# A hybrid decoder layer: the steps of w_down's second half at which turned tiles are taken apart and put together

## The chip, the core and the metric

The kernel runs on one core of a Trainium2 chip. The metric is the device time of one execution in microseconds (us). TensorE multiplies matrices, VectorE and ScalarE work on tiles element by element, GpSimd is used here for a few transfers, and SyncE issues most transfers (DMAs). Each engine works through its own instructions in order, and semaphores tie the engines together.

## What is computed

The layer holds 256 tokens of width 2048. A mixer (chunked SSD scan beside dilated attention) comes first; the change lies in the last product of the MLP behind it. What matters of the reference:

```
def squared_relu_mlp(u, w_up, w_down):
    hdn = jax.nn.relu(jnp.einsum('bsd,df->bsf', u, w_up))
    return jnp.einsum('bsf,fd->bsd', hdn * hdn, w_down)
...
        ff = squared_relu_mlp(rmsnorm(h, norm_mlp_pre[i]), w_up[i], w_down[i])
        h = h + rmsnorm(ff, norm_mlp_post[i])
```

The hidden width is 8192. The kernel takes it in two halves of 4096: w_up's half first, then the rows of w_down that belong to it.

## The kernel before, in words

**Products in two parts.** A float32 operand is split into a high part, which ScalarE rounds (`split`, L150, tiles `hi`), and the rest, which VectorE subtracts (L151, tiles `lo`). TensorE then forms hi·hi, lo·hi and hi·lo. Weights pass through five `hi` and five `lo` buffers (`BUFS = 5`), so that a split can be written only when TensorE is through with the one five splits before.

**Units and steps.** `unit` forms two blocks of 512 columns of w_down at a time. It takes the inner dimension in steps of two 128-row tiles. A plain step fetches two weight tiles, splits two, and feeds 24 matmuls of 512 columns. A step "by seven" (`seven`) does a 2x2 block product with seven products in place of eight: it has four splits, three additions of weights on VectorE, and 21 matmuls. It also needs sums of activations (`sums_of_acts`, three additions or subtractions with the names `r<-r` and a split with the name `ua<-r`), which are made one step ahead. The first unit of w_down's second half has the order 0, 1, 3, 2, 6, 4, 5, 8, 7, 9, 10, 11, 12, 13 of inner pairs, where 3, 6, 8, 9, 11 and 13 go by seven. In steps counted from 0: steps 2, 4, 7, 9, 11 and 13 go by seven, the others are plain. After step 13 the last two pairs (14 and 15) follow as plain ones; I call them the last steps.

**Turned tiles.** The blocks of w_up leave tokens on the partitions, and w_down needs features there. Each of the four blocks that the last unit of w_up leaves is therefore turned (`turned`) in two parts. Taking it apart: ScalarE applies relu and square (L1522, L1523) and writes the 16-bit halves apart (L1515, `ha<-hb` or `ha<-wpost`, 128x1024), and SyncE issues a transposing DMA (L1525). Putting it together, called landing here: ScalarE joins the halves again (L1515, `ha<-hb` or `ha<-wpost`, 128x2x512) and rounds the result (L150, `ah_3798`), and VectorE subtracts (L151, `al_3799`). Two tuples say at which steps of a unit this stands: `TURNS` before the step's own work, `LANDS` after it. In w_down's units both parts are placed exactly: `in_line` orders them after the splits recorded so far.

**What follows the last landing.** When no turned tile is left, `more_in_place` runs: the tile of the halves becomes a further place for fetched weights (`ha`), and two rows of norm weights are loaded. The weights of the last steps begin with that place, so their first fetch waits for the fourth landing, and three more are chained behind it.

Of the kernel before, what the change touches and what calls it, by code (L numbers as in the profile page):

```python
# [54 lines left out]
V_SEVENS = (1, 3, 5, 6)  # L55
QK_SEVENS = (1, 3, 5, 6)
PAIRS_AHEAD = 4
TURNS = ((1, 2, 4, 5), (3, 4, 8, 9))
LANDS = ((0, 3, 4, 6), (0, 6, 7, 10, 11))


def constants():
# [18 lines left out]
def hymba_layer(ctx: ExitStack, tc: tile.TileContext, x, norm_mix_pre, w_in, conv_w, conv_b, dt_bias, a_log,  # L81
# [99 lines left out]
    room = {}  # L181
# [13 lines left out]
    def beside_up(raws, turn, halves=None):  # L195

        room["sums"] = [v[:, k:k + KB] for k in range(0, NK // 2, KB) for v in att[1]]
        b = hp.tile([P, NT, NB], F32, name="hb")
        room["shared"] = [[b[:, t] for t in range(NT)],
                          [hp.tile([P, NB], F32, name="wpost", bufs=2) for _ in range(NT)]]  # L200
        room["last"] = deque([room["shared"][1].pop(), hp.tile([P, NB], F32, name="junk")])
        room["shared"][1].append(room["last"][0])
        a = hp.tile([P, 3 * KB, NB], F32, name="ha")
        in_a = [a[:, k:k + KB] for k in range(0, 3 * KB, KB)]
        halves = in_a.pop(0) if halves is None else halves
        room["halves"] = deque(halves[:, i].bitcast(U16) for i in range(KB))
        room["raw"], room["turn"], room["acts"], room["chain"] = [*raws, *in_a], turn, act_u, True
        room["of_halves"], room["of_a"] = halves, in_a
        sums_of.clear()

    def beside_down():

        a = hp.tile([P, 3 * KB, 2, S], F32R, name="ha")
        room["sums"] = [a[:, k] for k in range(3 * KB)]
        room["raw"], room["turn"], room["acts"] = [mws[2]], 0, part
        room["halves"] = deque(mws[0][:, t, c0:c0 + NB].bitcast(U16) for t in range(NT) for c0 in (0, NB))
        room["then"] = [(4, halves_beside_down), (2, more_beside_down), (0, all_beside_down)]
        sums_of.clear()

# [65 lines left out]
    def blocks_of(n):  # L285
        return n if isinstance(n, tuple) else (n * NB, (n + 1) * NB)
# [57 lines left out]
    def drain():  # L344
        while waiting:
            pump()
# [3 lines left out]
    def pump_beside(exact=False):  # L350

        if not beside:
            return
        work = beside.popleft()
        room["exact"] = exact
        with tc.issue_after(newest["act"].ins):
            next(work)
        flying.append(work)

    def land_beside(exact=False):  # L360

        room["exact"] = exact
        if flying:
            with tc.issue_after(newest["act"].ins):
                next(flying.popleft(), None)
        if "then" in room and len(beside) + len(flying) <= room["then"][0][0]:
            room["then"].pop(0)[1]()
            if not room["then"]:
                room.pop("then")
# [49 lines left out]
    def sums_of_acts(k):  # L419

        if k in sums_of:
            return sums_of[k]
        places = room["sums"][2 * len(sums_of):][:2]
        h_, l_, r = room["acts"](k * KB)
        with tc.high_priority(offset=AHEAD):
            a, c = (tmp().rearrange("p (i s) -> p i s", s=P) for _ in range(2))
            ah_, al_ = (v[:, r:r + KB].bitcast(F32).rearrange("p j (t s) -> p j t s", t=NT) for v in (h_, l_))
            nc.vector.tensor_tensor(a.rearrange("p (j t) s -> p j t s", t=NT), ah_, al_, op=ALU.add)
            nc.vector.tensor_tensor(c[:, 0:2], a[:, 0::3], a[:, 1:2].to_broadcast([P, 2, P]), op=ALU.subtract)
            nc.vector.tensor_tensor(c[:, 2], a[:, 0], c[:, 1], op=ALU.add)  # L430
            nc.vector.tensor_tensor(c[:, 3], a[:, 2], c[:, 2], op=ALU.subtract)
            ch, cl = (v.rearrange("p b (t s) -> p (b t) s", t=NT) for v in places)
            split(ch, cl, c)
        sums_of[k] = ch, cl
        return ch, cl

    def seven(src, ca, cb, k, acc, more, first, last):


        ch, cl = sums_of_acts(k)  # L440
        h_, l_, r = room["acts"](k * KB)
        with tc.high_priority(offset=AHEAD):
            raw_a = fetch_next(src, k * KB, ca)
            raw_b = fetch_next(src, k * KB, cb, pair_of(src, ca, k))
            e, t4 = sum_tile(), tmp()
            add_in_line(e[:, 1], raw_a[:, 0], raw_b[:, 0])
            add_in_line(e[:, 0], e[:, 1], raw_b[:, 1], ALU.subtract)
            hl_a = parts()
            split_in_line(*hl_a, raw_a)
            add_in_line(t4, e[:, 1], raw_a[:, 1])  # L450
            hl_e = parts()
            split_in_line(*hl_e, e)
            hl_b = parts()
            split_in_line(*hl_b, raw_b)
            hl_t = parts()
            split_in_line(*(v[:, 0] for v in hl_t), t4)

        def block(j, t):
            return tuple(v[:, r + j, t * P:(t + 1) * P] for v in (h_, l_))

        def summed(i):
            return ch[:, i], cl[:, i]

        for dst, (a_h, a_l), (hi, lo), j, own in (
                (more[0], block(0, 0), hl_a, 0, True), (acc[0], block(1, 0), hl_a, 1, False),
                (more[1], summed(1), hl_e, 0, True), (more[2], summed(2), hl_e, 1, True),
                (more[3], summed(0), hl_b, 0, True), (acc[1], summed(3), hl_b, 1, False),
                (acc[2], block(1, 1), hl_t, 0, False)):
            nc.tensor.matmul(dst, a_h, hi[:, j], start=own and first, stop=False)  # L469
            nc.tensor.matmul(dst, a_h, lo[:, j], start=False, stop=False)  # L470
            nc.tensor.matmul(dst, a_l, hi[:, j], start=False, stop=own and last)  # L471
# [30 lines left out]
    def unit(src, n, order, last, acc, more, combine, lag=0, at_end=(None, None), first=True, ending=None,  # L502
             ready=None, halves=None):


        cols = blocks_of(n)
        sevens = [k for k, by_seven in order if by_seven]
        for i, (k, by_seven) in enumerate(order):
            if i in TURNS[len(order) > 7]:
                pump_beside(len(order) > 7)  # L510
            if i + 1 < len(order) and order[i + 1][1]:
                sums_of_acts(order[i + 1][0])
            if by_seven:
                if k == sevens[0]:
                    drain()
                    if ready:
                        ready()
                seven(src, *cols, k, acc, more, k == sevens[0], k == sevens[-1])
            else:
                for b in range(2):  # L520
                    row_tiles(src, cols[b], [k], acc[b::2], room["acts"], first and i == 0, False,
                              fetch=fetch_next)
            if i in LANDS[len(order) > 7]:
                land_beside(len(order) > 7 and i > 0)
            if k == sevens[-1]:
                combine(more)
        for b in range(2):
            if b and ending:
                ended.append(ending(cols[b], last, acc))
            else:  # L530
                row_tiles(src, cols[b], last, acc[b::2], room["acts"], False, True, lag if b else 0, at_end[b],
                          fetch=fetch_last if b else fetch_next, halves=halves if b else None)
# [956 lines left out]
    def out_of_place():  # L1489

        yield from copies(in_dram, of_h, 4)
        beside_up([*tiles_of(mws[0], (0, NB)), mws[2]], -2 * RAWS, mws[1])
        for k in UP_SEVENS:
            sums_of_acts(k)
            yield
# [73 lines left out]
    def complete(n):  # L1569
        def at_end(t, acc):  # L1570
            m = mw_at(t, columns(n))
            nc.vector.tensor_add(m, acc, m)
            junk = hp.tile([P, NB], F32, name="junk")
            nc.scalar.activation(junk, m, AF.Square, accum_out=ssq[:, t, n:n + 1])
            nc.vector.tensor_mul(m, m, wpost[n])
            if n == 2:
                first3[t] = sums_but_last(ssq, t)
        return at_end
# [6 lines left out]
    def more_in_place():  # L1585
# [5 lines left out]
        for n in range(2):  # L1591
            load_wpost(norm_mlp_post, n)

    room["then"] = [(0, more_in_place)]
    unit(w_downs[1], 0, orders[("down", 1), 0], (14, 15), acc, more,
         lambda x: combine_onto(0, x), 0, (complete(0), complete(1)))
    room["chain"] = False
# [36 lines left out]
```

## Time and profile before

| | us |
|---|---|
| median of 3 runs (1441.72 to 1447.8) | 1443.69 |
| the profiled execution | 1444.83 |
| its span in the trace | 1442.9 |
| TensorE busy in it | 1432.2 (99%) |

The span is the time from the first to the last instruction in the trace; the profiled execution's own time has 1.93 us around it. Busy time of TensorE counts matmuls that overlap in its pipeline: each lasts 0.39 us and they start about 0.23 us apart, so a matmul that starts late shows as a larger distance between starts before it shows as idle time.

### The profile page before, as it was taken

How to read it: one execution, taken by the hardware profiler on the slowest of the kernel's cores; microseconds unless marked ns; L12 is line 12 of the kernel's file. 1: busy time of each engine (PE TensorE's matmuls, PEld its weight loads, DVE VectorE, ACT ScalarE, POOL GpSimd, SP SyncE). 2: the span in 40 equal slices, each digit the busy share in tenths (PEclk: the TensorE clock that was granted, in tenths of full speed). 3: DMA queues.
4: the chain of work that ended last, by engine and by line, in shares of the span. 5: the costliest groups of instructions: out<-in, count | busy, mean ns of one | idle time of the engine just before them, and what ended most of it. 6: DMA issues, size and time to landing. Idle time of an engine off the chain costs nothing.

```text
span 1442.9 us, 20235 instructions
## 1 busy us (share of the span) xinstructions
PE 1432.2 (99%) x6930; PEld 1204.6 (83%) x6930; DVE 1297.6 (90%) x1881; ACT 1003.1 (70%) x1407; POOL 162.8 (11%) x244
## 2 busy tenths in 40 slices
PE   9999999999999999999999999999999999999998
PEld 8888888888888888888888888888888888887886
DVE  7788888988999778689988999999889999999998
ACT  7577669666666666656667669978565799978664
POOL 0301110121111000011100011010111011111000
PEclk9999999999999999999999999999999999999999
DMA  8977656756888648588976799799888899998954
GB/s 266 282 211 227 188 171 184 246 176 193 220 244 259 198 119 253 176 259 261 274 230 218 203 340 291 206 253 254 256 251 272 253 266 298 247 274 251 323 194 146
DMA packets 201926, 340.30 MB, mean 236 GB/s; under 512 B 45616, under 2 KB 48544, under 8 KB 201824
## 3 DMA queue, kind: packets, MB, share of 16 engines
q1 hardware_dynamic: 174304, 279.72, 61.7%
q0 software_dynamic: 19648, 45.63, 15.5%
q10 hardware_dynamic: 7872, 13.68, 2.9%
q8 instruction: 54, 0.88, 0.2%
q14 instruction: 48, 0.39, 0.1%
HBM read 327.39 MB, written 49.84 MB: 261 GB/s over the span
## 4 chain that ended last, share of the span: by engine, by line
PE 64%; DVE 5%; ACT 4%; DMA 2%; issue 2%; SPq 0%; ACTq 0%; DVEq 0%
PE acc L383 9%; PE acc L384 9%; PE acc L382 9%; PE acc L470 5%; PE acc L471 5%; PE acc L469 5%; PE acc L540 4%; PE ps L383 2%; PE ps L384 2%; PE ps L382 2%; PE acc L543 2%; ACT hi L150 2%; DVE lo L151 2%; PE ps L469 2%; PE ps L470 2%
## 5 line engine op out<-in xcount | busy, mean ns | idle before, releaser
L151 DVE TENSOR_TENSOR lo<-raw,hi 128x1024 fp32r<-128x1024 f32 (+1 forms) x390 | 473.2, 1218 | 79.0 <-ACT hi L150 77.2
L150 ACT ACTIVATE hi<-raw 128x1024 fp32r<-128x1024 f32 (+1 forms) x390 | 406.5, 1048 | 174.1 <-PE acc L384 51.2
L540 PE MATMUL acc<-ua,hi 128*128 128x512 f32 x520 | 141.2, 400 | 0.0
L150 ACT ACTIVATE hi<-e 128x1024 fp32r<-128x1024 f32 x66 | 69.9, 1059 | 53.6 <-DVE e L275 49.9
L540 PEld LDWEIGHTS acc<-ua,hi 128*128 128x128 f32 x520 | 91.3, 189 | 14.0
L382 PE MATMUL acc<-hi,ua 128*128 128x512 f32 x228 | 90.0, 395 | 0.0
L383 PE MATMUL acc<-lo,ua 128*128 128x512 f32 x228 | 89.2, 391 | 0.0
L384 PE MATMUL acc<-hi,ua 128*128 128x512 f32 x228 | 89.0, 390 | 0.0
L382 PE MATMUL acc<-hi,sh 128*128 128x512 f32 x220 | 86.7, 394 | 0.0
L383 PE MATMUL acc<-lo,sh 128*128 128x512 f32 x220 | 85.7, 390 | 0.0
L384 PE MATMUL acc<-hi,sl 128*128 128x512 f32 x220 | 85.7, 389 | 0.0
L543 PEld LDWEIGHTS acc<-ua,lo 128*128 128x128 f32 x520 | 76.5, 189 | 8.9
L151 DVE TENSOR_TENSOR lo<-e,hi 128x1024 fp32r<-128x1024 f32 x66 | 80.4, 1218 | 0.9 <-ACT hi L150 0.7
L543 PE MATMUL acc<-ua,lo 128*128 128x256 f32 x520 | 78.8, 281 | 0.0
L470 PE MATMUL acc<-lo,ah 128*128 128x512 f32 x180 | 70.1, 390 | 0.0
L471 PE MATMUL acc<-hi,al 128*128 128x512 f32 x180 | 70.0, 389 | 0.0
L469 PE MATMUL acc<-hi,ah 128*128 128x512 f32 x180 | 70.0, 389 | 0.0
L151 DVE TENSOR_TENSOR lo<-ha,hi 128x1024 fp32r<-128x1024 f32 x48 | 58.3, 1219 | 3.7 <-ACT hi L150 3.5
L540 PE MATMUL acc<-uc,hi 128*128 128x512 f32 x208 | 61.4, 405 | 0.0
L150 ACT ACTIVATE hi<-ha 128x1024 fp32r<-128x1024 f32 x48 | 50.3, 1050 | 9.4 <-PE acc L384 5.7
L469 PE MATMUL acc<-hi,ua 128*128 128x512 f32 x137 | 53.5, 390 | 0.0
L471 PE MATMUL acc<-hi,ua 128*128 128x512 f32 x137 | 53.3, 389 | 0.0
(578 smaller groups left out, 3724.7 us busy)
## 6 DMA issues: line engine op xcount, KB each, us to landing
raw<-in_w_in_dram SPq DMA_DIRECT2D x154, 512.0 KB, 4.4
raw<-in_w_down_dram SPq DMA_DIRECT2D x70, 512.0 KB, 5.7
raw<-in_w_up_dram SPq DMA_DIRECT2D x65, 512.0 KB, 4.8
raw<-in_w_out_dram SPq DMA_DIRECT2D x38, 512.0 KB, 5.3
raw<-pair SPq DMA_DIRECT2D x59, 256.0 KB, 4.5
pair<-in_w_up_dram POOLq DMA_DIRECT2D x56, 256.0 KB, 6.4
pair<-in_w_down_dram POOLq DMA_DIRECT2D x52, 256.0 KB, 6.0
ha<-in_w_up_dram SPq DMA_DIRECT2D x25, 512.0 KB, 6.0
```

The source lines that it names most:

```text
L150: return (nc.scalar.activation(hi, src, AF.Copy), nc.vector.tensor_tensor(lo, src, hi.bitcast(F32), op=ALU.subtract))
L151: nc.vector.tensor_tensor(lo, src, hi.bitcast(F32), op=ALU.subtract))
L382: nc.tensor.matmul(dst[:, cs], a_h[:, r, ts], hi[:, j, cs], start=begin and j == 0, stop=False)
L383: nc.tensor.matmul(dst[:, cs], a_h[:, r, ts], lo[:, j, cs], start=False, stop=False)
L384: product[t] = nc.tensor.matmul(dst[:, cs], a_l[:, r, ts], hi[:, j, cs], start=False, stop=end and j == KB - 1)
L469: nc.tensor.matmul(dst, a_h, hi[:, j], start=own and first, stop=False)
L470: nc.tensor.matmul(dst, a_h, lo[:, j], start=False, stop=False)
L471: nc.tensor.matmul(dst, a_l, hi[:, j], start=False, stop=own and last)
L540: nc.tensor.matmul(acc[f], hi[:, j, f * P:(f + 1) * P], u(k0 + j), start=k0 + j == 0, stop=False, skip_group_check=True)
L543: nc.tensor.matmul(acc[f][:, 0], lo[:, j, f * P:(f + 1) * P], u(k0 + j)[:, 0], start=False, stop=k0 + j == NK - 1, skip_group_check=True)
```

## The change

A third pair of tuples is added for w_down's second half, and the unit chooses its pair by a number in `room` in place of the length of the order. Tiles one and two are taken apart at steps 3 and 4 as before, tiles three and four at steps 9 and 10 in place of 8 and 9. The landings stand behind steps 7, 8, 11 and 12 in place of 6, 7, 10 and 11. The units of w_up keep the first pair and those of w_down's first half the second.

```diff
-TURNS = ((1, 2, 4, 5), (3, 4, 8, 9))
-LANDS = ((0, 3, 4, 6), (0, 6, 7, 10, 11))
+TURNS = ((1, 2, 4, 5), (3, 4, 8, 9), (3, 4, 9, 10))
+LANDS = ((0, 3, 4, 6), (0, 6, 7, 10, 11), (0, 7, 8, 11, 12))
...
-        room["of_halves"], room["of_a"] = halves, in_a
+        room["of_halves"], room["of_a"], room["table"] = halves, in_a, 0
...
+        room["table"] = 1
...
+        table = room.get("table", 0)
...
-            if i in TURNS[len(order) > 7]:
-                pump_beside(len(order) > 7)
+            if i in TURNS[table]:
+                pump_beside(table > 0)
...
-            if i in LANDS[len(order) > 7]:
-                land_beside(len(order) > 7 and i > 0)
+            if i in LANDS[table]:
+                land_beside(table > 0 and i > 0)
...
+    room["table"] = 2
     unit(w_downs[1], 0, orders[("down", 1), 0], (14, 15), acc, more,
```

TensorE and GpSimd have the same instructions in the same order as before. Three places show how the others move. From line 209 on the changed kernel's line numbers are one, two or three higher than before (L275 becomes L276, L1515 becomes L1517, L1522 becomes L1524).

First, VectorE at the start of step 7 (`raw` are its weights, `e` their sums), before:

```order
L430 TENSOR_TENSOR r<-r 128x128
L151 TENSOR_TENSOR lo<-raw,hi 128x1024
L431 TENSOR_TENSOR r<-r 128x128
L151 TENSOR_TENSOR al_3799<-ha,ah_3798 128x4x128
L275 TENSOR_TENSOR e<-raw 128x512
L275 TENSOR_TENSOR e<-e,raw 128x512
L151 TENSOR_TENSOR ua<-r,ua 128x512
L151 TENSOR_TENSOR lo<-raw,hi 128x1024
L275 TENSOR_TENSOR r<-e,raw 128x512
```

and with the change:

```order
L431 TENSOR_TENSOR r<-r 128x128
L151 TENSOR_TENSOR lo<-raw,hi 128x1024
L432 TENSOR_TENSOR r<-r 128x128
L276 TENSOR_TENSOR e<-raw 128x512
L276 TENSOR_TENSOR e<-e,raw 128x512
L151 TENSOR_TENSOR ua<-r,ua 128x512
L151 TENSOR_TENSOR lo<-raw,hi 128x1024
L276 TENSOR_TENSOR r<-e,raw 128x512
```

The subtraction of the first landing (`al_3799`) no longer stands ahead of step 7's additions; it comes after its last split, beyond these rows.

Second, ScalarE from the last split of step 7 (`hi<-r`) to the first of step 9 (`hi<-ha`); the two `hi<-uc` are those of step 8. Before:

```order
L150 ACTIVATE hi<-r 128x512
L1515 ACTIVATE ha<-hb 128x2x512
L150 ACTIVATE ah_3798<-ha 128x4x128
L1522 ACTIVATE wpost<-wpost,rmlp 128x512
L1523 ACTIVATE wpost<-wpost 128x512
L150 ACTIVATE ua<-r 128x512
L1515 ACTIVATE ha<-wpost 128x1024
L150 ACTIVATE hi<-uc 128x1024 x2
L1522 ACTIVATE wpost<-wpost,rmlp 128x512
L1523 ACTIVATE wpost<-wpost 128x512
L1515 ACTIVATE ha<-wpost 128x1024
L150 ACTIVATE hi<-ha 128x1024
```

With the change:

```order
L150 ACTIVATE hi<-r 128x512
L1517 ACTIVATE ha<-hb 128x2x512
L150 ACTIVATE ah_3798<-ha 128x4x128
L150 ACTIVATE ua<-r 128x512
L150 ACTIVATE hi<-uc 128x1024 x2
L1517 ACTIVATE ha<-hb 128x2x512
L150 ACTIVATE ah_3798<-ha 128x4x128
L1524 ACTIVATE wpost<-wpost,rmlp 128x512
L1525 ACTIVATE wpost<-wpost 128x512
L1517 ACTIVATE ha<-wpost 128x1024
L150 ACTIVATE hi<-ha 128x1024
```

Before, the second landing and the taking apart of the third tile stand ahead of step 8's splits; now the first landing stands there, and the second landing and the third tile follow them, ahead of step 9's. The fourth tile is taken apart between step 9's splits and step 10's.

Third, VectorE at the fourth landing, where `lo<-uc` are the splits of step 12 and `e<-ha` begins step 13. Before:

```order
L151 TENSOR_TENSOR lo<-r,hi 128x512
L151 TENSOR_TENSOR al_3799<-ha,ah_3798 128x4x128
L428 TENSOR_TENSOR r<-ah_3798,al_3799 128x512
L151 TENSOR_TENSOR lo<-uc,hi 128x1024
L429 TENSOR_TENSOR r<-r 128x256
L151 TENSOR_TENSOR lo<-uc,hi 128x1024
L430 TENSOR_TENSOR r<-r 128x128
```

With the change:

```order
L151 TENSOR_TENSOR lo<-r,hi 128x512
L429 TENSOR_TENSOR r<-ah_3798,al_3799 128x512
L151 TENSOR_TENSOR al_3799<-ha,ah_3798 128x4x128
L430 TENSOR_TENSOR r<-r 128x256
L151 TENSOR_TENSOR lo<-uc,hi 128x1024
L431 TENSOR_TENSOR r<-r 128x128
L151 TENSOR_TENSOR lo<-uc,hi 128x1024
L432 TENSOR_TENSOR r<-r 128x128
L151 TENSOR_TENSOR al_3799<-ha,ah_3798 128x4x128
L276 TENSOR_TENSOR e<-ha 128x512
```

The fourth landing's subtraction has moved behind both splits of step 12. SyncE's queue from there, before (from the third transposing DMA):

```order
L1525 DMA_TRANSPOSE wpost<-ha 128x8x128
L164 DMA uc<-in_w_down_dram 128x2x512 x2
L1525 DMA_TRANSPOSE wpost<-ha 128x8x128
L164 DMA ha<-in_w_down_dram 128x2x512
L159 DMA ha<-pair_93 128x512
L160 DMA ha<-in_w_down_dram 128x512
L164 DMA ha<-in_w_down_dram 128x2x512
L164 DMA raw<-in_w_down_dram 128x2x512 x4
L164 DMA uc<-in_w_down_dram 128x2x512 x2
```

With the change (from the two fetches into `uc` for step 12):

```order
L164 DMA uc<-in_w_down_dram 128x2x512 x2
L1527 DMA_TRANSPOSE wpost<-ha 128x8x128
L164 DMA ha<-in_w_down_dram 128x2x512
L159 DMA ha<-pair_93 128x512
L160 DMA ha<-in_w_down_dram 128x512
L1527 DMA_TRANSPOSE wpost<-ha 128x8x128
L164 DMA uc<-in_w_down_dram 128x2x512 x2
L164 DMA ha<-in_w_down_dram 128x2x512
L164 DMA raw<-in_w_down_dram 128x2x512 x4
```

The third and the fourth transposing DMA have each moved behind fetches, and the two `uc` fetches of the next unit have moved ahead of the `ha` fetch and the `raw` fetches of the last steps, which wait for the fourth landing.

## Rows read from the trace of the kernel before

**Rows 1.** The page, part 1: busy time and share of the span of each engine.

```profile
PE 1432.2 (99%) x6930; PEld 1204.6 (83%) x6930; DVE 1297.6 (90%) x1881; ACT 1003.1 (70%) x1407; POOL 162.8 (11%) x244
```

**Rows 2.** Windows: busy us per engine (instructions), granted TensorE clock, DMA share, GB/s.

```profile
1294.00:1306.50 12.50, 12.50 (x56) 10.13 (x54) 9.98 (x17) 10.20 (x13) 1.36 (x2) 1.00 1.11 332
1306.50:1316.40 9.90, 7.66 (x26) 5.78 (x26) 8.09 (x9) 8.32 (x10) 1.49 (x3) 0.83 1.02 279
1316.40:1341.50 25.10, 25.10 (x112) 20.81 (x111) 24.61 (x36) 20.27 (x23) 2.03 (x3) 1.00 0.82 240
318.00:330.00 12.00, 11.14 (x69) 9.50 (x68) 10.99 (x19) 11.07 (x27) 5.46 (x7) 1.00 0.46 130
```

**Rows 3.** Timeline of TensorE: start, duration, instruction, idle before and its releaser.

```profile
1306.27 0.39 PE L471 MATMUL ps<-hi,al 128*128 128x512 f32 x1
...
1308.15 0.51 PE L382 MATMUL ps<-hi,sh 128*128 128x512 f32 x1 [1.49 <-ACT hi L150]
...
1309.41 0.50 PE L383 MATMUL ps<-lo,sh 128*128 128x512 f32 x1 [0.76 <-DVE lo L151]
...
1310.78 0.63 PE L382 MATMUL ps<-hi,sh 128*128 128x512 f32 x1
...
1311.21 0.63 PE L383 MATMUL ps<-lo,sh 128*128 128x512 f32 x1
...
1316.37 0.39 PE L469 MATMUL acc<-hi,ah 128*128 128x512 f32 x1
...
1341.53 0.62 PE L382 MATMUL ps<-hi,ah 128*128 128x512 f32 x2
```

**Rows 4.** Timeline of ScalarE, the splits of steps 7 to 9.

```profile
1294.17 1.37 ACT L1515 ACTIVATE ha<-hb 128x1024 uint16<-128x1024 uint16 x1 [2.73 <-DMA hb<-ha]
...
1301.23 1.37 ACT L1515 ACTIVATE ha<-hb 128x1024 uint16<-128x1024 uint16 x1
...
1303.17 0.71 ACT L1522 ACTIVATE wpost<-wpost,rmlp 128x512 f32<-128x512 f32 x1
...
1305.58 0.63 ACT L150 ACTIVATE ua<-r 128x512 fp32r<-128x512 f32 x1 [1.03 <-DVE r L431]
...
1306.11 1.04 ACT L1515 ACTIVATE ha<-wpost 128x1024 uint16<-128x1024 uint16 x1
...
1307.06 1.99 ACT L150 ACTIVATE hi<-uc 128x1024 fp32r<-128x1024 f32 x2
...
1308.95 0.71 ACT L1522 ACTIVATE wpost<-wpost,rmlp 128x512 f32<-128x512 f32 x1
...
1311.32 1.04 ACT L150 ACTIVATE hi<-ha 128x1024 fp32r<-128x1024 f32 x1
```

**Rows 5.** Timeline of VectorE, around the first landing and at the last split.

```profile
1294.21 0.28 DVE L431 TENSOR_TENSOR r<-r 128x128 f32<-128x128 f32 x1
...
1296.24 0.69 DVE L151 TENSOR_TENSOR al<-ha,ah 128x512 fp32r<-128x512 f32 x1 [1.75 <-ACT ah L150]
...
1296.85 0.69 DVE L275 TENSOR_TENSOR e<-raw 128x512 f32<-128x512 f32 x1
...
1340.30 1.22 DVE L151 TENSOR_TENSOR lo<-ha,hi 128x1024 fp32r<-128x1024 f32 x1
```

**Rows 6.** Timeline of SyncE: the fetch behind the fourth landing.

```profile
1329.07 0.38 SPq L164 DMA_DIRECT2D ha<-in_w_down_dram  x1
```

**Rows 7.** DMA issues from 1282, 1275, 1329.0 and 1329.4 us: median us to landing last.

```profile
hb<-ha SPq DMA_TRANSPOSE x1, 11.7
...
raw<-in_w_down_dram SPq DMA_DIRECT2D x2, 512.0 KB, 11.4
...
ha<-in_w_down_dram SPq DMA_DIRECT2D x1, 512.0 KB, 4.7
...
raw<-in_w_down_dram SPq DMA_DIRECT2D x3, 512.0 KB, 8.1
```

**Rows 8.** Timeline of TensorE: a short wait in an earlier stage.

```profile
320.62 0.71 PE L865 MATMUL ps<-cT 128*128 128x128 f32 x4 [0.64 <-ACT bn L871]
```

## The prediction

> **What bounds the kernel now.** I read the page first: TensorE is busy in 99% of the span [rows 1], so time can come only from places where its matmuls start late, or be lost by new ones. Matmuls last 0.39 us but start closer together, so I looked at the distances between starts in w_down's second half. From 1316.37 to 1341.53, steps 9 to 13, there are 21+24+21+24+21 = 111 matmuls in 25.16 us, or 0.2267 us each: full pace [rows 3]. In the stretch that the change touches I find one place that is not at this pace, the start of step 8. The last matmul of step 7 starts at 1306.27, so step 8 is due at 1306.50 and step 9, after 24 x 0.2267 = 5.44 us, at 1311.94; step 9 starts at 1316.37 [rows 3]. The loss is 4.43 us. Of it, the first matmul waits 1.65 us for ScalarE's hi and the second 1.03 for VectorE's lo (1309.41 - 1308.15 - 0.23); the other 1.75 us come after them, where starts stand 0.43 us apart, half pace, with 0.83 of the clock granted over the stretch [rows 2, 3].
>
> Then I followed the wait back. Step 8's splits (`hi<-uc`) start on ScalarE only at 1307.06. Ahead of them stand the second landing (1301.23 to 1303.17: 1.94 us), relu, square and the halves of the third tile, and a wait of 1.03 us for VectorE's activation sums [rows 4]. Further back, at 1294.17, ScalarE had waited 2.73 us for the first tile's transposing DMA, which took 11.7 us to land, and VectorE, whose next instruction was that landing's subtraction, had idled 1.75 us [rows 4, 5, 7]. So the stall begins with a landing that came before its data. After the stall, from 1316.4 to 1341.5, VectorE is busy 24.61 of 25.10 us [rows 2]; there it is as close to the limit as TensorE. This is what keeps the gain small.
>
> **The change part by part.** No instruction is added or dropped, so every price is one of place. Step lengths on TensorE: 5.44 us plain, 21 x 0.2267 = 4.76 us by seven. Step 7 starts at 1301.74 as before.
>
> *The first landing leaves step 6's end.* VectorE can begin step 7's additions right after 1294.21, at about 1294.4, in place of 1296.85: 2.4 us earlier [rows 5]. ScalarE's last split of step 7 then waits for a buffer: the one that TensorE frees halfway through step 6, which starts at 1296.30; 2.72 us later plus some 0.2 to finish is 1299.2. The landing follows a half-size split by 0.53 us (1305.58 to 1306.11) [rows 4], so it stands at 1299.75 to 1301.7, well after its data (1294.2). The wait for the sums, which ended at 1305.58, ends 2.4 us earlier and another 0.6 because a landing's subtraction (1296.24 to 1296.85, rows 5) no longer stands ahead of them: 1302.6. Step 8's first split starts 0.53 later, 1303.1, against 1307.06. Its hi is ready at 1304.2 and its lo some 1.2 us later, 1305.4; they are wanted at 1306.50 and 1306.73. I count the stall of 4.43 us as gone, with 1.3 us to spare.
>
> *The second landing and the third tile move behind step 8's splits.* On ScalarE: 1303.1, two splits 1.9 us, landing 1.94, taking apart 2.37 (1308.95 to 1311.32) [rows 4], so step 9's first split starts at 1309.3, lo at about 1311.6; wanted at 1311.94 + 0.23 = 1312.17. It holds by 0.5 us. VectorE meanwhile idles some 1.3 us, because it has nothing to subtract until that split.
>
> *The fourth tile moves between the splits of steps 9 and 10.* Step 9's four splits take about 3 x 0.95 + 0.53 = 3.4 us, the fourth tile 2.37, so step 10's first split starts at 1315.1, its hi is ready at 1316.2, its lo at 1317.5. TensorE wants that lo at 1316.70 + 0.23 = 1316.9. A new wait of about 0.6 us opens here: ScalarE is what is late, with VectorE behind it.
>
> *From step 10 on VectorE sets the pace.* Before, its stream from step 10's first lo (after a hi that starts when TensorE's first matmul of step 9 is under way, about 1316.6, and takes 1.06: 1317.7) to the last steps' first lo (1340.30, rows 5) was 22.6 us, with about 0.5 idle [rows 2]. With the change it starts at 1316.25 and holds the same work: 1316.25 + 22.1 = 1338.4, done 1.22 later at 1339.6 [rows 5]. TensorE wants this lo one matmul into the last steps, so these begin at about 1339.4 in place of 1341.53. The gain is 2.1 us; the other 2.3 of the stall are given back in waits of 0.5 to 0.8 us at steps 10, 12 and the last ones. The same from the other side: VectorE idled 2.52 + 1.81 + 0.49 = 4.82 us from 1294 to 1341.5 [rows 2], and any gain up to the last steps must come out of that. My walk leaves it idle 2.4 us (0.3 and 0.6 around step 8's splits, 1.3 before step 9's, 0.2 later), which gives 2.4. I take 2.2. The bounds are 0 (all given back) and 4.43 (nothing given back).
>
> *The fourth landing moves behind step 12's splits, and a fetch behind it.* The `ha` fetch of the last steps went out at 1329.07, when the landing's subtraction was over [rows 6]. This now comes two full splits and some sums later in VectorE's stream, 3.4 us, less the 2.2 gained: about 1330.4. It took 4.7 us to land, the three behind it 8.1 [rows 7]. At 4.7 it is there at 1335.1, at 8.1 at 1338.5; with 1.06 for hi, the lo wanted at 1338.4 is late by nothing or by 1.2. SyncE now sends two `uc` fetches ahead of it, which speaks for the later figure, but the DMA share there is 0.82, against 1.11 when the slow ones were under way [rows 2], which speaks for the earlier. I cost it at nothing, hidden behind VectorE's own backlog.
>
> *The rest.* The third and fourth transposing DMAs keep two steps, over 10 us, between taking apart and landing (9 to 11 and 10 to 12 in place of 8 to 10 and 9 to 11), and the fetches queued behind them on SyncE are for steps two or more ahead. The norm rows load later, long before their use. The second unit uses the new tuples with nothing left to turn. I cost these at nothing.
>
> **The clock.** After the stall the granted clock fell and TensorE ran at half pace, 1.2 GHz, which is the 1.75 us above. In an earlier stage with a single wait of 0.64 us it stayed at 1.00 [rows 2, 8]. My new waits are of that size, so I expect 2.4 GHz throughout. The Trainium skill (TensorE: Matmul & The Clock Gate, "A second HAM failure mode: psum-queue depth-cycling") says that frequent short idles between groups of matmuls can make the clock go back and forth and cost the pace; by that rule three short waits would be worse than they look, and the row of the earlier stage does not bear it out for one wait alone.
>
> **The rivals.**
> *The stall goes and nothing comes back.* This needs ScalarE to be 0.6 us faster than my walk before step 10 and VectorE to find 2 us of slack; the 24.61 of 25.10 speak against it. It gives -4.4: 1439.3.
> *The stall only moves.* The new wait before step 10 is as long as the old, or another transfer is late in place of the first. ScalarE's 9.9 us between 1303.1 and step 10's split have no cover; 2 us more there give 0: 1443.7.
> *Slower: the fetch behind the fourth landing.* If it takes what the worst pair took, 11.4 us [rows 7], it lands at 1341.8, its lo is ready at 1344.1, and the last steps begin at 1343.9, 2.4 us later than before; with a fallen clock another 1.75: +4.2, 1447.9. It decides from 7 us of landing on (1330.4 + 7 + 1.06 = 1338.4), and turns a gain into a loss from about 9.
> *Short waits that drop the clock.* Each of three short waits followed by a half-pace stretch like the one that lost 1.75 us would take the 2.2 back and add up to 3: about 1443.2 for one, 1446.7 for three.
>
> **How the numbers follow.** The profiled execution took 1444.83 us; 2.2 less is 1442.6. The median of the runs shown is 1.14 lower, 1443.69, and my forecast is made on that: 1441.5. Chances: forecast 0.55, nothing comes back 0.12, only moves 0.18, slow fetch 0.09, clock 0.06. The runs of before scatter from 2 below to 4 above their median, so the range reaches past the cases' own: 1437.5 to 1446.5 leaves out most of the slow fetch and little else. Half a per cent, about what a measurement of this kernel can tell from no change, is 7.2 us, more than any case here moves it: within it 0.93, faster by more 0.04, slower by more 0.03.
>
> **What would show it.** Right: step 8 follows step 7 at 0.23 us, ScalarE has no wait for `hb<-ha`, step 9 starts about 4.4 us earlier than before, the last steps only about 2, with waits for VectorE or ScalarE under 1 us at step 10 and later and the clock at 1.00. Wrong: a wait of several us for the `ha` fetch at the last steps, a second stretch at half pace, or the last steps starting 4 us earlier with VectorE still at 98%.

## The result, and the profile after

The changed kernel takes 1448.84 us (median of 19 runs, 1447.25 to 1453.75) beside 1444.65 us for the kernel before (19 runs, 1441.46 to 1451.65). The ratio is 1.0027, with a 95% interval of 1.0016 to 1.0038: 4.2 us slower by the medians, where 2.2 us faster was forecast, and above the range. The profiled execution took 1453.75 us, with a span of 1451.8 us; it lost some time by chance in an earlier stage, of which the last section tells.

First the place of the old stall, TensorE at the end of step 7 and the start of step 8 (timeline: start, duration, instruction, idle before and its releaser):

```profile
1307.94 0.39 PE L470 MATMUL acc<-hi,ah 128*128 128x512 f32 x1
...
1312.48 0.39 PE L472 MATMUL ps<-hi,al 128*128 128x512 f32 x1
1312.70 0.39 PE L383 MATMUL ps<-hi,sh 128*128 128x512 f32 x1
1312.93 0.39 PE L384 MATMUL ps<-lo,sh 128*128 128x512 f32 x1
```

Step 7 starts at 1307.94, and step 8 follows its last matmul at 0.22 us, with no wait; before, the distance was 1.88 us, the next 1.26, and half pace came after them [rows 3]. ScalarE in the same stretch answers [rows 4]:

```profile
1306.01 1.36 ACT L1517 ACTIVATE ha<-hb 128x1024 uint16<-128x1024 uint16 x1
...
1308.46 2.10 ACT L150 ACTIVATE hi<-uc 128x1024 fp32r<-128x1024 f32 x2
...
1314.77 1.04 ACT L150 ACTIVATE hi<-ha 128x1024 fp32r<-128x1024 f32 x1
```

The landing at 1306.01 has no wait for `hb<-ha` any more. Step 8's splits begin 0.52 us after step 7 does (1308.46 - 1307.94), where it was 5.32 us (1307.06 - 1301.74) before.

Now the end of the unit. TensorE from step 13 into the last steps:

```profile
1343.68 0.39 PE L472 MATMUL ps<-hi,al 128*128 128x512 f32 x1
1345.68 0.73 PE L383 MATMUL ps<-hi,ah 128*128 128x512 f32 x2 [1.62 <-ACT hi L150]
1348.38 0.80 PE L383 MATMUL acc<-hi,ah 128*128 128x512 f32 x1 [1.97 <-ACT hi L150]
1348.97 0.63 PE L384 MATMUL ps<-lo,ah 128*128 128x512 f32 x1
...
1353.61 0.40 PE L384 MATMUL ps<-lo,ah 128*128 128x512 f32 x1
```

The last steps were due at 1343.68 + 0.23 = 1343.91, and start 1.77 us late. After two matmuls TensorE waits again: 2.70 us from 1345.68 to 1348.38, of which two matmuls take 0.45, so 2.25 us are lost. The twelve distances between the starts from 1348.38 to 1353.61 add up to 5.23 us in place of 2.72: half pace, 2.51 us more. The sum is 6.53 us. ScalarE tells what is waited for:

```profile
1344.57 1.06 ACT L150 ACTIVATE hi<-ha 128x1024 fp32r<-128x1024 f32 x1 [3.79 <-DMA ha<-in_w_down_dram]
1345.93 1.06 ACT L150 ACTIVATE hi<-raw 128x1024 fp32r<-128x1024 f32 x1 [0.30 <-DMA raw<-in_w_down_dram]
1347.27 1.06 ACT L150 ACTIVATE hi<-raw 128x1024 fp32r<-128x1024 f32 x1 [0.28 <-DMA raw<-in_w_down_dram]
```

It stands idle for 3.79 us until the `ha` fetch of the last steps has landed, and then waits for each of the fetches behind it. The first matmul of the last steps needs the first of these splits, and the third matmul (`acc<-hi`, the second block's first) needs the third, which ends at 1348.33. SyncE issued the fetch here (SPq is its queue), which answers [rows 6]:

```profile
1333.76 1.81 SPq L164 DMA_DIRECT2D uc<-in_w_down_dram  x2
1335.90 0.37 SPq L164 DMA_DIRECT2D ha<-in_w_down_dram  x1
1336.32 4.47 SPq L164 DMA_DIRECT2D raw<-in_w_down_dram  x4
```

DMA issues of this and of the first transposing DMA, with KB and median us to landing, against 4.7 and 11.7 us in [rows 7]:

```profile
ha<-in_w_down_dram SPq DMA_DIRECT2D x1, 512.0 KB, 8.7
...
hb<-ha SPq DMA_TRANSPOSE x1, 8.9
```

Last the windows (busy us per engine with instructions, granted TensorE clock, DMA share, GB/s) of step 7 with what leads to it, of step 8, of steps 9 to 13 and of the last steps, against [rows 2]:

```profile
1300.20:1312.70 12.50, 12.50 (x56) 10.32 (x56) 11.15 (x16) 9.29 (x11) 2.17 (x3) 1.00 1.03 335
1312.70:1318.10 5.40, 5.40 (x25) 4.50 (x24) 4.07 (x6) 5.28 (x7) 0.55 (x1) 1.00 0.94 249
1318.10:1343.90 25.80, 25.52 (x112) 20.44 (x111) 25.18 (x35) 18.89 (x23) 2.16 (x3) 1.00 0.85 199
1343.90:1354.00 10.10, 6.52 (x17) 4.76 (x17) 8.34 (x10) 5.81 (x6) 0.55 (x1) 0.66 1.03 386
```

The fallen clock has moved from step 8 (0.83 in [rows 2]) to the last steps (0.66). Up to there this profile gains more than the change was to gain: from the start of step 7 the last steps are due after 1343.91 - 1307.94 = 35.97 us, where they began after 1341.53 - 1301.74 = 39.79 us before. All of that and more is lost behind 1343.91.

### The profile page after: what moved, and what is told of

Read it like the earlier page. It is cut to its first block, busy times and chain, and to the rows that moved or that the text cites. A ratio compares the mean times of both kernels' runs of the same rounds, so it can differ in the third digit from the quotient of the medians.

```text
span 1451.8 us, 20237 instructions
## 1 busy us (share of the span) xinstructions
PE 1437.2 (99%) x6930; PEld 1206.7 (83%) x6930; DVE 1298.2 (89%) x1881; ACT 1003.0 (69%) x1407; POOL 162.4 (11%) x244
## 4 chain that ended last, share of the span: by engine, by line
PE 61%; DVE 6%; ACT 5%; DMA 3%; issue 3%; SPq 0%; ACTq 0%; DVEq 0%
PE acc L383 8%; PE acc L385 8%; PE acc L384 8%; PE acc L471 5%; PE acc L472 5%; PE acc L470 5%; PE acc L542 4%; DVE lo L151 3%; ACT hi L150 2%; PE acc L545 2%; PE ps L384 2%; PE ps L385 2%; PE ps L383 2%; PE ps L470 2%; PE ps L472 2%
```

## The experiments

For each profile I give two losses against full pace, which is 21 x 0.2267 us for a step by seven and 24 x 0.2267 for a plain one: from the start of step 2 to that of step 13 (56.46 us at full pace), and from step 13 to the next unit's first step by seven (26.52 us), which takes in the last steps and the two plain ones behind them. Before has 4.41 and 0.00, the changed kernel 0.58 and 6.55.

The theory from the profile: the fourth landing comes later, so the `ha` fetch comes later too, and the two `uc` fetches of the next unit now stand ahead of it, so that it takes 8 us and more in place of 4.7 to 6. The rivals: the early landings' new order costs the time in some way that the profile hides; the tile that became a place for weights is to blame; TensorE's own order at the last steps, in which the second block's first matmul comes third, is to blame.

**Two halves of the change.** `first_two` delays the first two landings alone, `last_two` the last two landings and the last two takings apart.

```diff
# first_two
-TURNS = ((1, 2, 4, 5), (3, 4, 8, 9), (3, 4, 9, 10))
-LANDS = ((0, 3, 4, 6), (0, 6, 7, 10, 11), (0, 7, 8, 11, 12))
+TURNS = ((1, 2, 4, 5), (3, 4, 8, 9), (3, 4, 8, 9))
+LANDS = ((0, 3, 4, 6), (0, 6, 7, 10, 11), (0, 7, 8, 10, 11))
# last_two
-LANDS = ((0, 3, 4, 6), (0, 6, 7, 10, 11), (0, 7, 8, 11, 12))
+LANDS = ((0, 3, 4, 6), (0, 6, 7, 10, 11), (0, 6, 7, 11, 12))
```

> Only the first two landings are late (steps 7 and 8); the other two and all the taking apart stand as before (lands 0, 7, 8, 10, 11; turns 3, 4, 8, 9). Theory: step 8 starts on time as in the changed kernel, the ha fetch goes out in time and ScalarE has no wait over 1 us for it; the last steps start 2 to 4 us earlier than before: ratio 0.997 to 0.999, about 1441.5. Rival (late step of w_up belongs to the change, or short waits cost the clock): 1447 or more.

> Only the second pair is moved (turns 3, 4, 9, 10; lands 0, 6, 7, 11, 12). Theory: the stall of step 8 stays (about 4.4 us with the half pace behind it) and the last steps wait for the ha fetch too, though by less, since TensorE comes to them later: 2 to 6 us on top, ratio 1.002 to 1.004. Rival (the fetch is late only because TensorE arrives 4.4 us earlier): no wait at the last steps, ratio 1.000.

`first_two` gave a ratio of 1.0009 (0.9998 to 1.0021), `last_two` 1.0003 (0.9993 to 1.0014). Neither came where I had it: the half that was to hold the gain shows none, and the half that was to hold the loss shows little of it. (1.0003 is what the rival of `last_two` had, but its ground, that nothing waits at the last steps, does not hold either.) Their traces say why. In `first_two` step 8 still waits, and ScalarE shows for what:

```profile
1305.30 0.64 ACT L150 ACTIVATE ua<-r 128x512 fp32r<-128x512 f32 x1 [1.11 <-DVE r L432]
1305.84 0.71 ACT L1524 ACTIVATE wpost<-wpost,rmlp 128x512 f32<-128x512 f32 x1
1306.58 0.63 ACT L1525 ACTIVATE wpost<-wpost 128x512 f32<-128x512 f32 x1
1307.25 1.06 ACT L1517 ACTIVATE ha<-wpost 128x1024 uint16<-128x1024 uint16 x1
1308.21 1.99 ACT L150 ACTIVATE hi<-uc 128x1024 fp32r<-128x1024 f32 x2
```

The third tile's taking apart, 2.37 us from 1305.84 to 1308.21, stands ahead of step 8's splits. TensorE was due at 1308.87 and started at 1309.31, and its second matmul came 1.26 us behind in place of 0.23: 1.5 us lost by these two waits, without half pace behind them. Beyond step 12 I can't set this trace beside the others step by step, since TensorE's order differs there; over both stretches it loses 3.6 us.

`last_two` loses nothing up to step 13, although its first landing is early and ScalarE waits 0.75 us for the transposing DMA: the third tile no longer stands in front. Its queue on SyncE is that of the changed kernel, its `ha` fetch takes 7.6 us, and it loses 1.77 us at the last steps, without half pace. (The profile puts ScalarE's wait for that split down to TensorE there, but the split begins at 1339.89, just when the fetch has landed, 1332.22 + 7.6.) There TensorE's order is plain, the second block after the first; that difference to the changed kernel led to `in_turn` below.

**The same kernel once more**, to see what of its profile repeats.

> The changed kernel itself, once more. Theory (the fetch behind the fourth landing): ScalarE waits some 3.8 us for the ha fetch of the last steps, these start about 4 us late with a stretch at half pace, step 8 follows step 7 without a wait; time about 1448.8, ratio to before 1.002 to 1.004. The late step of w_up at 1262 us in the first profile is chance by this theory and need not be there again. Rival (the loss of 3.9 us at that step of w_up belongs to the change, although no instruction ahead of it moved): it is there again at the same step, and the wait at the last steps alone does not account for the ratio.

The ratio was 1.0028 (1.0015 to 1.0041). The losses are 1.56 and 6.20 us; TensorE (at step 10 too) and ScalarE at the last steps:

```profile
1317.64 0.39 PE L383 MATMUL ps<-hi,ah 128*128 128x512 f32 x1
1318.48 0.50 PE L384 MATMUL ps<-lo,ah 128*128 128x512 f32 x1 [0.45 <-DVE lo L151]
...
1340.49 0.73 PE L383 MATMUL ps<-hi,ah 128*128 128x512 f32 x2 [0.96 <-ACT hi L150]
1343.10 0.79 PE L383 MATMUL acc<-hi,ah 128*128 128x512 f32 x1 [1.88 <-ACT hi L150]
```

```profile
1339.38 1.06 ACT L150 ACTIVATE hi<-ha 128x1024 fp32r<-128x1024 f32 x1 [3.15 <-DMA ha<-in_w_down_dram]
```

Both long waits are there, in the same places, and so is the stretch at half pace behind them. Step 10, at 1317.64, has the wait for VectorE's lo that the prediction had put there: 0.84 us to the next start, 0.61 more than full pace.

**The fetches in their old order.** `chained` keeps the rule of `fetch_next` (L242) that a fetch goes behind those recorded before it for as long as the unit's end is recorded too, so the two `uc` fetches of the next unit go behind the `ha` and `raw` fetches. `chained_again` is the same kernel, timed once more.

```diff
     unit(w_downs[1], 0, orders[("down", 1), 0], (14, 15), acc, more,
          lambda x: combine_onto(0, x), 0, (complete(0), complete(1)))
-    room["chain"] = False
 
     def onto_and_h(more):
+        room["chain"] = False
```

> The changed kernel, but the fetches of the next unit stay chained, so that SyncE sends the ha fetch and the raw fetches of the last steps ahead of the two uc fetches, as before the change. If the two uc fetches in front make the ha fetch slow (8.65 us to land in place of 4.7): it lands in 4.5 to 6 us, the wait of ScalarE falls from 3.8 to 0 to 1.5 us, time 1443 to 1445. If it is only the late issue behind the fourth landing: the wait stays above 2.5 us and the time at 1447 to 1449.

> The same kernel as chained, for a second interval. If its gain is the change's own, as forecast, the ratio is 0.998 to 0.9995 again with the ha fetch in 4.7 to 6 us; if 0.9988 was chance, 0.9995 to 1.001.

The ratios were 0.9988 (0.9978 to 0.9999) and 1.0000 (0.9990 to 1.0011), so the loss is gone both times; the second lies where its expectation had put chance, so a gain is not shown. The losses are 1.36 and 0.03 us, and 1.55 and 0.47. SyncE and ScalarE of `chained`:

```profile
1331.73 0.38 SPq L164 DMA_DIRECT2D ha<-in_w_down_dram  x1
1332.17 2.61 SPq L164 DMA_DIRECT2D raw<-in_w_down_dram  x4
1334.82 1.04 SPq L164 DMA_DIRECT2D uc<-in_w_down_dram  x2
```

```profile
1336.98 1.06 ACT L150 ACTIVATE hi<-ha 128x1024 fp32r<-128x1024 f32 x1 [0.84 <-DMA ha<-in_w_down_dram]
```

The `ha` fetch takes 5.2 us, and its split begins 2.79 us ahead of the last steps (1339.77). It is issued no earlier than in the changed kernel: 8.04 us ahead of them here, 8.01 there (1343.91 - 1335.90). The second row of norm weights, 256 KB on ScalarE's queue, is sent 0.6 us ahead of it in both kernels (1331.15 and 1335.31), so that transfer does not make the difference. How fast fetches land behind each other can be read where ScalarE waits for nothing but them, at the last steps of the changed kernel: the splits there start 1.36 and 1.34 us apart (1344.57, 1345.93, 1347.27). Two fetches ahead are therefore worth some 2.7 us, an estimate from these rows, and 5.2 and 2.7 are 7.9, close to the 8.0 to 8.7 us that the changed kernel shows.

**The other ways to have the fetch early.** `first_two_newturn` puts the last two landings back behind steps 10 and 11, `turns_only` all four back. `no_place` leaves the landings of the change, but the tile does not become a place for weights, so no fetch waits for the fourth landing.

```diff
# first_two_newturn
-LANDS = ((0, 3, 4, 6), (0, 6, 7, 10, 11), (0, 7, 8, 11, 12))
+LANDS = ((0, 3, 4, 6), (0, 6, 7, 10, 11), (0, 7, 8, 10, 11))
# turns_only
-LANDS = ((0, 3, 4, 6), (0, 6, 7, 10, 11), (0, 7, 8, 11, 12))
+LANDS = ((0, 3, 4, 6), (0, 6, 7, 10, 11), (0, 6, 7, 10, 11))
# no_place
-        room["turn"] %= RAWS + len(room["raw"])
-        room["raw"].append(room["of_halves"])
```

> Landings 7, 8, 10, 11 and taking apart at 3, 4, 9, 10: the first two landings and the third and fourth tile late, the last two landings as before; SyncE sends the ha fetch ahead of the two uc fetches. Theory (only the order of those fetches behind the last landing costs time; the late taking apart of the third tile frees step 8): step 8 on time, no wait for the ha fetch, under 2 us lost from step 2 to the next unit, ratio 0.997 to 0.999. Rival (with the landings so close behind the taking apart, ScalarE and VectorE are crowded at steps 9 to 11): waits of 1 us and more there, ratio 1.000 or above.

> Taking apart at 3, 4, 9, 10 as in the change, all landings as before (6, 7, 10, 11). Theory (step 8's stall of before comes at least as much from the third tile's taking apart in front of its splits as from the early landing): step 8 loses less than 1.5 us although ScalarE may still wait for the first transposing DMA; ratio 0.998 to 1.000. Rival (the early landing alone makes the stall): step 8 still loses 3 to 4.5 us, ratio 0.999 to 1.001.

> The changed kernel, but the tile of the halves does not become a place for fetched weights, so no fetch of the last steps waits for the fourth landing (one place fewer from there on). Theory: no wait of ScalarE for a fetch over 1 us at the last steps, ratio 0.998 to 1.000, unless the missing place makes later fetches late. Rival (the last steps are late for VectorE's sake, not for the fetch): they start 2 us or more late all the same, 1.002 or more.

The ratios were 1.0002 (0.9991 to 1.0013), 0.9991 (0.9981 to 1.0001) and 0.9996 (0.9985 to 1.0006). None loses anything at the last steps (0.00, 0.00 and 0.02 us), and up to step 13 they lose 1.80, 2.33 and 1.74. `turns_only` and `no_place` came as their theories had it; `first_two_newturn` lost as little as its theory said, and TensorE stands idle for no more than 0.5 us at a time in its steps 9 to 12, but its ratio is in the rival's range. In the first two the scheduler itself sends the `uc` fetches after the others, with `ha` landing in 5.4 and 6.1 us; they are ahead only where the fourth landing is late. `first_two_newturn` has TensorE's instructions at the last steps in the changed kernel's order, the second block's matmul in third place:

```profile
1339.28 0.39 PE L472 MATMUL ps<-hi,al 128*128 128x512 f32 x1
1339.51 0.61 PE L383 MATMUL ps<-hi,ah 128*128 128x512 f32 x2
1339.96 0.39 PE L383 MATMUL acc<-hi,ah 128*128 128x512 f32 x1
1340.19 0.39 PE L384 MATMUL ps<-lo,ah 128*128 128x512 f32 x1
```

With the fetch in time that order costs nothing. `turns_only` says something of the old stall: with all landings where they were, and only the third and fourth tile taken apart a step later, step 8 follows step 7 without a wait (at 0.23 us), in its one profile.

**TensorE's order alone.** `chained` had changed that order too, since the scheduler sets it by when it expects operands. So `in_turn` takes the changed kernel, with SyncE as it is, and holds the row tiles of the last steps in the order in which they are written.

```diff
-                    row_tile(acc[t], t, held[at], ks[at], acts, first and at == 0, last and at == n - 1)
+                    with tc.issue_after(product[1 - t].ins) if last and room.get("chain") else ExitStack(): row_tile(acc[t], t, held[at], ks[at], acts, first and at == 0, last and at == n - 1)
```

The changed kernel begins its last steps with `ps<-hi` twice, then `acc<-hi`, then `ps<-lo` (`ps` is the first block, `acc` the second). `in_turn` begins them with `ps<-hi`, `ps<-lo`, `ps<-hi,al`, and its first `acc` comes behind the whole first block, at 1348.11; `chained` has the same order.

> The kernel with the change, with TensorE's last steps forced into the plain order (first block's tokens 0 and 1, then the next pair, then the second block), which is the order that TensorE has in chained; SyncE, and VectorE and ScalarE up to there, as in the changed kernel, the two uc fetches ahead of the ha fetch. Theory A (the late fetch is the cause, and the early place of the second block's first matmul makes it dearer, since TensorE then waits for the second raw fetch too): ha still takes 7.5 to 8.7 us, ScalarE waits some 3 us for it, TensorE loses 1.5 to 3.5 us at the last steps in place of 6.2, ratio 1.000 to 1.0015. Theory B (TensorE's order is nothing, the fetch alone costs it all): as the changed kernel, loss 6 to 6.5 us, ratio 1.002 to 1.004. Theory C (TensorE's order is the cause and the fetch is not): like chained, no loss over 1 us at the last steps, ratio 0.998 to 0.9995.

The ratio was 1.0016 (1.0006 to 1.0025), just above theory A's range and below B's. The losses are 1.36 and 2.60 us, and the second is in A's range alone. TensorE:

```profile
1339.89 0.39 PE L472 MATMUL ps<-hi,al 128*128 128x512 f32 x1
1341.50 0.49 PE L383 MATMUL ps<-hi,ah 128*128 128x512 f32 x1 [1.23 <-ACT hi L150]
1342.76 0.50 PE L384 MATMUL ps<-lo,ah 128*128 128x512 f32 x1 [0.77 <-DVE lo L151]
1343.10 0.40 PE L385 MATMUL ps<-hi,al 128*128 128x512 f32 x1
1343.34 0.39 PE L383 MATMUL ps<-hi,ah 128*128 128x512 f32 x1
```

```profile
1340.39 1.06 ACT L150 ACTIVATE hi<-ha 128x1024 fp32r<-128x1024 f32 x1 [3.42 <-DMA ha<-in_w_down_dram]
```

The fetch is as late as in the changed kernel (8.3 us, and ScalarE waits 3.42 us for it), but TensorE loses 1.38 and 1.03 us and goes on at full pace. So the late fetch by itself costs 2.4 us by these two waits. `chained` and `in_turn` have TensorE's last steps in the same order and differ in the queue: 0.03 and 0.47 us lost against 2.60. `in_turn` and the changed kernel have the same queue and differ in TensorE's order: 2.60 against 6.55 and 6.20. The early matmul of the second block, which waits for a split two fetches further on, adds the rest together with the half pace that follows. Neither is enough without the late fetch.

**The kernel before, profiled once more**, to have its old stall twice.

> The kernel before, a second profile. If the stall of step 8 belongs to it in most executions: 3 to 4.5 us lost there again, with a wait of ScalarE for the first transposing DMA. If it hangs on how long that DMA takes in a run: a landing under 9.5 us goes with a loss under 2 us.

It took 1445.42 us, with 3.70 and 0.00 us lost. The stall stands at step 8 again, with 1.18 and 1.26 us from start to start, half pace behind, and a first transposing DMA of 11.0 us. Both profiles of the kernel before are 1.1 and 1.6 us above the medians of the runs taken with them (1443.69 and 1443.79).

**How usual that stall is.** For most runs the record has the granted clock over the whole span. Five of the twelve profiles have a stretch at half pace before the kernel's last microseconds: both of the kernel before, both of the changed kernel, and `last_two`, by chance at about 980 us (0.83 over 975 to 985). These five show 0.996 to 0.998 over the span; the other seven show 0.999 or 1.000. Of 87 timed runs of the kernel before, 12 show 0.998 or less, with a median of 1445.9 us, and 75 show 0.999 or more, with 1443.4. So both profiles of the kernel before are of the rarer kind, and in most of its executions there is no half pace behind step 8. The last column counts the runs at 0.998 or less: 28 of 31 of the changed kernel and 3 of 12 of `in_turn`, so the half pace goes with the early matmul far more often than with the late fetch alone.

| kernel | ratio | lost to step 13 | at the last steps | `ha` fetch, us | TensorE there | runs with clock 0.998 or less |
|---|---|---|---|---|---|---|
| before, first and second profile | 1 | 4.41, 3.70 | 0.00, 0.00 | 4.7, 6.0 | second block third | 12 of 87 |
| changed, first and second profile | 1.0027, 1.0028 | 0.58, 1.56 | 6.55, 6.20 | 8.7, 8.0 | second block third | 28 of 31 |
| in_turn | 1.0016 | 1.36 | 2.60 | 8.3 | plain | 3 of 12 |
| last_two | 1.0003 | -0.02 | 1.77 | 7.6 | plain | 5 of 12 |
| first_two | 1.0009 | 3.6 with the last steps | | 5.5 | not compared | 0 of 12 |
| first_two_newturn | 1.0002 | 1.80 | 0.00 | 5.4 | second block third | 0 of 12 |
| turns_only | 0.9991 | 2.33 | 0.00 | 6.1 | plain | 0 of 12 |
| no_place | 0.9996 | 1.74 | 0.02 | none | plain | 0 of 12 |
| chained, both | 0.9988, 1.0000 | 1.36, 1.55 | 0.03, 0.47 | 5.2, 5.8 | plain | 0 of 24 |

## Why the prediction was wrong, and where it was right

**The stall of step 8: right, for more than one reason.** In the traces the 4.43 us are gone, in both profiles and all variants that move the third tile; most executions of the kernel before did not have them in full, of which the sum below tells. Step 8's first split stands 0.52 us after step 7's start, where I had walked to 1.36. But I named the early landing as the beginning of the stall. `turns_only` and `last_two` keep it there and have no stall, and `first_two` moves it and still has one of 1.5 us, each in one profile. Ahead of step 8's splits the third tile's taking apart counted at least as much as the landing.

**Waits of 0.5 to 0.8 us at step 10 and step 12, VectorE giving back 2.3: right, a little too dear.** At step 10 the changed kernel shows none and 0.61 us, `chained` 0.61; at step 12 all three show 0.4. In `chained`, where nothing disturbs the end, the last steps begin 36.77 us after step 7 in place of 39.79, 3.0 us earlier where I had 2.1. I had expected VectorE to idle 2.4 us in place of 4.82 up to there; in `chained` the window from 1295.26 to 1339.77, which begins as far ahead of step 7 as the one from 1294.00 did, gives 44.51 - 41.99 = 2.52:

```profile
1295.26:1339.77 44.51, 43.80 (x192) 35.38 (x191) 41.99 (x58) 36.06 (x42) 4.88 (x7) 1.00 0.90 242
```

**The fetch behind the fourth landing: the step that failed.** "I cost it at nothing, hidden behind VectorE's own backlog." The issue was about where I put it: 9.0 us ahead of the last steps by my walk (1330.4 and 1339.4), 8.0 us by the trace (1343.91 - 1335.90). The point from which it decides came out right, though by two terms that were each 1 us off: the first matmul starts 1.11 us after its split begins (1345.68 - 1344.57), where I had left 2.0, so of 8.0 us 6.9 are left for the transfer, and I had 7. What was wrong is the time that I took for the transfer, and its price: nothing by my sum, 2.6 us by `in_turn` with TensorE's order out of play, and 6.2 to 6.5 us in the changed kernel. Of my two bounds, 4.7 and 8.1 us, I took the lower, arguing with the share of busy DMA engines, 0.82 against 1.11. That is a mean over a stretch of 25 us; the fetch met two others of 512 KB that had been sent in the 2.1 us ahead of it. The Trainium skill (DMA: Bandwidth & Descriptors, "Queues, rings and completion order") says that each DMA engine takes the descriptors of a queue in their order; the traces agree, 7.6 to 8.7 us behind two fetches and, in both profiles of `chained`, 5.2 and 5.8 in front of them. The order of the queue was in front of me, and the fetches were named as speaking for the later figure, but I weighed a mean against it.

The price at 8.1 us was 1.2 us for the late lo. By the first matmul that was nearly right: 1.77 and 1.12 us in the two profiles. Not seen were the other two parts: the third matmul, which waits for the third split (2.25 and 2.16 us), and the half pace after it (2.51 us in the first profile). TensorE's order had these instructions in the same sequence before the change, where the data were early and the order did not matter.

**The rival that came true** was the slow fetch, with a chance of 0.09 and a price of +4.2 us in sum. The measured difference is +4.2 too, but that is luck, as its parts are others: I had the last steps 2.4 us late and one half pace at a transfer of 11.4 us, and 8.0 to 8.7 us were enough to lose 6.2 to 6.5 there, against a gain ahead of them.

**The clock.** I expected 2.4 GHz throughout. The new short waits are as I had them: after 0.61 and 0.42 us at steps 10 and 12 the granted clock stays at 1.00 and the starts at 0.23 us, so the rival of the short waits fell. The half pace came with the long waits that I had not foreseen.

**The sum.** Without the late fetch the change's own effect is near what the walk gave in the profiles, 1.7 to 3.0 us less over both stretches in `chained`, but the timed runs don't confirm it: `chained` is 1.6 us below before by the medians of one comparison, and 0.8 above in the other. I made the sum against one profiled execution and then moved it to the median, as if the median lost the same 4.43 us at step 8. It does not: 75 of 87 runs of the kernel before show no stretch at half pace (above). What such a run loses from step 2 to the next unit can be estimated: it is a variant's loss in its profile, less the distance of its median above that of the kernel before in the same comparison. Over the ten timed series of changed kernels this rough estimate gives 0.8 to 3.0 us (1.75 - 0.92 in `last_two`, 1.39 + 1.64 in `chained`) in place of 4.41 and 3.70. So even with the fetch in time there was less to gain than I had counted. The version without the loss is as fast as the kernel before, and no version is shown to be faster.

## What to carry to other kernels

When a release moves later, follow the first transfer that waits for it to the queue that issues it, count what now stands ahead of it there, and price each by the distance at which transfers land behind each other; a mean DMA share over a stretch of 25 us told nothing of that here. Then ask which instruction of the consumer needs the last of a train of transfers, not the first: an order that is free while data come early multiplies a short delay when they come late. And a stall has all that stands ahead of the late instruction as its cause: see which part of it is enough to remove. Last, see whether the profiled execution is a usual one before its stall goes into a sum: here the granted clock of the other runs told that it was not.

## What was not expected of the hardware

Losses come by chance in code that the change leaves alone. In the first profile of the changed kernel the last step of w_up begins like this:

```profile
1261.67 0.39 PE L472 MATMUL acc<-hi,uc 128*128 128x512 f32 x1
1262.99 0.50 PE L383 MATMUL acc<-hi,uc 128*128 128x512 f32 x1 [0.93 <-ACT hi L150]
1264.25 0.50 PE L384 MATMUL acc<-lo,uc 128*128 128x512 f32 x1 [0.76 <-DVE lo L151]
...
1264.83 0.63 PE L383 MATMUL acc<-hi,uc 128*128 128x512 f32 x1
1265.25 0.63 PE L384 MATMUL acc<-lo,uc 128*128 128x512 f32 x1
```

Two waits of 1.1 and 1.0 us, half pace, and 3.9 us lost, while the second profile of the same kernel has nothing there. That is most of the 4.9 us between their spans (1451.8 and 1446.9), and more than the 2.2 us that were forecast.

Waits of almost the same length do and don't bring the half pace. Distances of 1.32 and 1.26 us did so here, and 1.18 and 1.26 at step 8 in the second profile of the kernel before; 1.61 and 1.26 in `in_turn` did not. The runs don't tell what else decides it.

The first transposing DMA took 8.6 to 12.3 us to land in these profiles, for the same 128x8x128 elements, and SyncE was held for 4.4 us by issuing it in the changed kernel:

```profile
1287.47 4.36 SPq L1527 DMA_TRANSPOSE hb<-ha  x1
1291.94 1.44 SPq L164 DMA_DIRECT2D uc<-in_w_down_dram  x2
...
1314.88 1.25 SPq L1527 DMA_TRANSPOSE wpost<-ha  x1
```

The two `uc` fetches behind it are issued only then. The size alone does not set this: the third transposing DMA, with as many elements, held SyncE for 1.25 us. The runs don't tell what makes the difference.
